# The list scheduler counts with half a microsecond more from the issue of a load to its landing

## The chip, the cores and the metric

The kernel runs on one core of a Trainium2 chip. The metric is the device time of one execution in microseconds (us), lower is better. Each time is that of a whole launch; the profile adds the span from the first to the last instruction of one execution.

## The reference

One inference step of a hybrid encoder layer in float32, for 2,048 prompt tokens and 32 sample tokens (2,080 columns together), width 1,024, feed-forward width 4,096.

```python
sh1, sc1, gt1, sh2, sc2, gt2 = jnp.split((silu(c) @ ada_w[l] + ada_b[l])[:, None, :], 6, axis=-1)
h = rmsnorm(x, norm_mix_g[l]) * (1 + sc1) + sh1
p = h @ w_in                      # u, v | q, k, v | z | a, b
a_out = u * (W_s v + b_s)         # gelu(u), rmsnorm(gelu(v)), chunks of 128 tokens
o, s_new = gated_delta_rule(q, k, vv, beta, g, s0)   # 4 heads, chunked, after a conv of width 4
b_out = rmsnorm(o, dn_norm_g) * silu(z)
x = x + gt1 * (jnp.concatenate([a_out, b_out], axis=-1) @ w_out)
h = rmsnorm(x, norm_ffn_g[l]) * (1 + sc2) + sh2
x = x + gt2 * (jnp.square(jax.nn.relu(h @ w_up[l])) @ w_down[l])
y = rmsnorm(x, final_norm_g)
```

## The kernel before

All large products are made as three matmuls: each float32 operand is split into a rounded high part and the remainder (`split`: ACT rounds, DVE subtracts), and high by high, high by low and low by high are summed in PSUM. A weight block arrives by a transfer into a raw buffer (`raw`, L1420; names `wr`, `s`), ACT writes its high part (`wh`, or `s` for the second feed-forward weight) with an ACTIVATE at L337, and DVE the low part (`wl`) with a TENSOR_TENSOR at L352. In what follows a **conversion** is such an ACT operation on a 128x512 block that a transfer brought, and an **eviction** is an ACT or DVE operation that reads a PSUM result of the feed-forward (names `f`).

The program runs through these stages: a start that makes the modulation from `ada_w` and the first projection (about 0 to 60 us), the mixers in two halves of 1,024 and 1,056 tokens (to about 1,035 us), and the feed-forward in four blocks of 520 tokens (`NB`), the first of which works out sums of weight quadrants (a Strassen scheme with seven products in place of eight) and stores them in DRAM as `su_d` and `sd_d`. Blocks 1 to 3, about 1,400 to 2,400 us, load those sums: 256 KB each, already split for the first weight (so ACT only rounds `wh` and `wl`), and not split for the second. Eight raw buffers of 256 KB serve the loads of blocks 1 to 3; a buffer comes free when ACT and DVE have read it.

No order of instructions is written by hand. Every operation is recorded with an engine, a cost, and what it reads and writes; `Program.schedule` (L237) then plays the program forward in a model of time and gives each engine a fixed order: at each free moment of an engine it takes, among the operations that are ready in the model, the one with the lowest key (priority class, then the earliest GEMM that depends on it). The engines then run these orders as queues: an operation that must wait holds up all that stand behind it on its engine. All transfers, loads and stores, are issued by SP (L390) in the scheduler's DMA order, and an issue whose buffer is not free yet holds up those behind it.

A transfer enters the model through `dma`: it takes the DMA lane for its bytes over 360 (in ns; at least 500), and what depends on it is ready `lat` later. The number that changes stands in `lat`:

```python
x = b / 360
self.p.op(DMA, max(500, x), ..., lat=DMA_LATENCY + min(0, x - 500))
...
s.ready = max(s.ready, end + o.lat + LATENCY.get((o.eng, s.eng), 0.0))
```

So for 256 KB (262,144 bytes) the model counts 728 + 3,000 = 3,728 ns from issue to landing, for 512 KB 4,456 ns, for the 130 KB of a 128x260 tile 3,370 ns. The same `lat` is counted for a store, before its buffer may be written again or its data loaded again.

Of the kernel before, what the change touches and what calls it, by code (L numbers as in the profile page):

```python
# [40 lines left out]
PE, DVE, ACT, POOL, DMA, NONE = range(6)  # L41
TABLES = {AF.Silu: "silu", AF.Gelu_apprx_tanh: "gelu", AF.Exp: "exp", AF.Ln: "ln"}

DMA_LATENCY = 3000


LATENCY = {(PE, DVE): 230, (PE, ACT): 230, (PE, POOL): 230, (DVE, PE): 380, (DVE, DVE): 130, (DVE, ACT): 160,
# [141 lines left out]
def R(x):  # L189
    return x.ap if isinstance(x, View) else x  # L190
# [132 lines left out]
class Kern:  # L323
# [61 lines left out]
    def dma(self, out, in_, n=None):  # L385
# [3 lines left out]
        x = b / 360  # L389
        self.p.op(DMA, max(500, x), lambda: nc.sync.dma_start(out=R(out), in_=R(in_)), [out], [in_], lat=DMA_LATENCY + min(0, x - 500))  # L390

# [1454 lines left out]
```

## Time and profile before

| what | value |
|---|---|
| median of 3 runs | 2415.27 us (2406.06 to 2415.52) |
| the profiled execution's own time | 2432.54 us |
| its span, first to last instruction | 2430.8 us |
| PE busy | 2363.7 us, 97% of the span |
| DVE, ACT, POOL busy | 1728.4, 1551.2, 757.9 us |
| moved by transfers | 570.38 MB, 235 GB/s on the mean |
| granted clock of PE | 0.996 of full |

The profiled execution took 17.27 us longer than the median run. PE is busy nearly throughout, so what another order can change is the 67.1 us of the span in which PE shows no work, and whatever new idle time it makes. Matmuls are pipelined and their ends are modelled, so gaps shorter than a matmul's own length are not seen as idle.

### The profile page before, as it was taken

The numbers are of one execution on the slowest core, as the hardware profiler recorded it, in microseconds if no ns is written. First come the engines' busy times: TensorE is split into PE (matmuls) and PEld (weight loads), VectorE is DVE, ScalarE is ACT, GpSimd is POOL, SyncE is SP. The second block draws the span as 40 slices with busy tenths as digits, with TensorE's granted clock in tenths as the row PEclk, the third lists the DMA queues.
The fourth block names the chain that finished last, engine by engine and source line by source line (L and its number), as shares of the span: only waits on it lengthen the run. The fifth ranks groups of instructions, "written<-read, shape, count | busy, mean of one in ns | idle before, by whom it ended". The sixth has DMA issues, their size and how long they took to land.

```text
span 2430.8 us, 53532 instructions
## 1 busy us (share of the span) xinstructions
PE 2363.7 (97%) x18834; PEld 2209.3 (91%) x18834; DVE 1728.4 (71%) x3993; ACT 1551.2 (64%) x3705; POOL 757.9 (31%) x1055
## 2 busy tenths in 40 slices
PE   7999999999999999999999999999999999999998
PEld 4877778999989878999999999999999999999998
DVE  5556666556664646477777778889788878878796
ACT  4555556465655435365554688777897877877774
POOL 2134523212433223444434353323431212511111
PEclk9999999999999999999999999999999999999999
DMA  8688668455557767888766778786888878876773
GB/s 302 212 280 301 199 192 262 136 180 163 149 167 218 240 189 240 267 266 257 274 217 218 256 245 275 235 292 231 271 284 275 273 237 263 256 251 224 244 232 111
DMA packets 387238, 570.38 MB, mean 235 GB/s; under 512 B 71356, under 2 KB 201296, under 8 KB 386968
## 3 DMA queue, kind: packets, MB, share of 16 engines
q1 hardware_dynamic: 386968, 566.96, 72.5%
q8 instruction: 148, 2.42, 0.4%
q14 instruction: 122, 1.00, 0.1%
HBM read 432.44 MB, written 134.35 MB: 233 GB/s over the span
## 4 chain that ended last, share of the span: by engine, by line
PE 55%; DMA 17%; ACT 9%; DVE 9%; issue 5%; POOL 3%; SPq 1%; DVEq 0%; POOLq 0%; ACTq 0%
PE f L398 25%; PE g L398 22%; DVE s L352 5%; ACT s L337 5%; DMA s<-su_d 4%; PE C L398 3%; POOL s L352 2%; DMA s<-w_u 2%; ACT wh L337 2%; PE B L398 2%; DVE wl L352 1%; DVE s L357 1%; PE L L398 1%; SPq L390 1%; ACT wl L337 1%
## 5 line engine op out<-in xcount | busy, mean ns | idle before, releaser
L337 ACT ACTIVATE s<-s 128x260 fp32r<-128x260 f32 (+9 forms) x1379 | 601.6, 463 | 300.4 <-DVE s L357 82.0
L398 PE MATMUL f<-s,s 128*128 128x260 f32 x4068 | 541.3, 283 | 6.5 <-DVE s L352 4.9
L352 POOL TENSOR_TENSOR s<-s,s 128x260 f32<-128x260 f32 (+3 forms) x354 | 358.5, 1024 | 532.7 <-ACT s L337 400.1
L398 PE MATMUL f<-BH,wh 128*128 128x260 f32 x1796 | 511.1, 285 | 12.7 <-DVE s L352 11.1
L398 PEld LDWEIGHTS f<-s,s 128*128 128x128 f32 x4068 | 508.7, 188 | 11.0 <-DVE s L352 7.2
L398 PE MATMUL f<-BH,wl 128*128 128x260 f32 x1796 | 507.7, 283 | 1.1 <-DVE wl L352 1.1
L398 PE MATMUL f<-BL,wh 128*128 128x260 f32 x1796 | 506.4, 282 | 0.1
L352 DVE TENSOR_TENSOR s<-s,s 128x512 fp32r<-128x512 f32 (+5 forms) x721 | 412.3, 586 | 97.6 <-ACT s L337 63.4
L398 PE MATMUL g<-BH,wh 128*128 128x512 f32 (+2 forms) x1112 | 422.2, 380 | 0.0
L352 DVE TENSOR_TENSOR s<-f,s 128x260 f32<-128x260 f32 x856 | 345.0, 420 | 97.9 <-PE f L398 90.3
L398 PE MATMUL g<-BH,wl 128*128 128x512 f32 (+2 forms) x1112 | 392.9, 353 | 0.0
L398 PE MATMUL g<-BL,wh 128*128 128x512 f32 (+2 forms) x1112 | 391.6, 352 | 0.6 <-DVE BL L352 0.6
L398 PEld LDWEIGHTS f<-BH,wh 128*128 128x128 f32 x1796 | 337.7, 188 | 16.7 <-DVE s L352 8.2
L398 PEld LDWEIGHTS f<-BH,wl 128*128 128x128 f32 x1796 | 338.2, 188 | 1.9 <-DVE wl L352 1.9
L398 PEld LDWEIGHTS f<-BL,wh 128*128 128x128 f32 x1796 | 338.5, 188 | 0.3 <-DVE BL L352 0.3
L352 POOL TENSOR_TENSOR s<-s 128x260 f32<-128x260 f32 (+11 forms) x315 | 155.2, 493 | 475.7 <-DVE s L352 239.5
L337 ACT ACTIVATE wh<-s 128x512 fp32r<-128x512 f32 (+1 forms) x369 | 230.3, 630 | 78.6 <-DMA s<-w_u 28.3
L398 PEld LDWEIGHTS g<-BH,wh 128*128 128x128 f32 x1112 | 211.1, 190 | 26.6 <-issue 9.5
L398 PEld LDWEIGHTS g<-BH,wl 128*128 128x128 f32 x1112 | 210.2, 189 | 19.4
L398 PE MATMUL f<-BH,s 128*128 128x260 f32 x1016 | 225.5, 284 | 0.9 <-DVE s L352 0.8
L398 PEld LDWEIGHTS g<-BL,wh 128*128 128x128 f32 x1112 | 211.1, 190 | 15.0 <-DVE BL L352 1.1
L357 DVE SCALAR_TENSOR_TENSOR s<-s,s,s 128x512 f32<-128x512 f32 (+6 forms) x318 | 164.2, 533 | 76.0 <-ACT s L337 38.4
(119 smaller groups left out, 3537.7 us busy)
## 6 DMA issues: line engine op xcount, KB each, us to landing
s<-su_d SPq DMA_DIRECT2D x288, 256.0 KB, 3.9
s<-w_u SPq DMA_DIRECT2D x171, 256.0 KB, 4.2
s<-w_d SPq DMA_DIRECT2D x151, 256.0 KB, 4.2
s<-sd_d SPq DMA_DIRECT2D x106, 256.0 KB, 4.1
wr<-su_d SPq DMA_DIRECT2D x96, 256.0 KB, 4.4
wr<-w_b SPq DMA_DIRECT2D x42, 512.0 KB, 4.7
wr<-w_d SPq DMA_DIRECT2D x70, 256.0 KB, 4.8
s<-x_d SPq DMA_DIRECT2D x128, 130.0 KB, 3.9
```

The costliest lines, as they stand in the source:

```text
L337: self.p.op(ACT, c, lambda: nc.scalar.activation(out=R(out), in_=R(in_), func=func, **{k: R(v) for k, v in kw.items()}), [out, accum], [in ...
L352: self.p.op(eng, c, lambda: e.tensor_tensor(out=R(out), in0=R(a), in1=R(b), op=op), [out], [a, b])
L357: self.p.op(DVE, c, lambda: nc.vector.scalar_tensor_tensor(out=R(out), in0=R(a), scalar=R(s), in1=R(b), op0=op0, op1=op1), [out], [a, s, b])
L390: self.p.op(DMA, max(500, x), lambda: nc.sync.dma_start(out=R(out), in_=R(in_)), [out], [in_], lat=DMA_LATENCY + min(0, x - 500))
L398: nc.tensor.matmul(R(out), R(l), R(r), **kw)
```

## The change

One constant. It changes the cost of no operation and takes none away; it moves the moment at which the scheduler holds a transfer's data to be there by 500 ns, for every transfer, and with it the order that each engine is given.

```diff
-DMA_LATENCY = 3000
+DMA_LATENCY = 3500
```

The model now counts 4,228 ns for 256 KB, 4,956 ns for 512 KB and 3,870 ns for 130 KB. All five engines' orders change; the instructions are the same ones, except that the change needs 37 loads of ACT's function tables where before has 39. From the first feed-forward eviction on, ACT has 1,011 operations on 128x512 blocks in both programs; the k-th of them stands behind 1.68 more of the other ACT operations in the change than in before, on the mean over all k.

The first place is on ACT, in block 1 of the feed-forward, the stretch that the trace shows from 1552 us on. `wl<-s_405`, `wh<-s_426` and `wl<-s_406` are conversions, `s_427<-s_427` are Relu and Square on a hidden tile, `BH_78<-...` is the split of such a tile, `s_427<-f_18035` is an eviction. Before:

```order
L337 ACTIVATE wl<-wr_96 128x512
L337 ACTIVATE s_411<-s_411,modc,a_90 128x260
L337 ACTIVATE wl<-s_405 128x512
L337 ACTIVATE s_427<-s_427 128x260
L337 ACTIVATE wh<-s_426 128x512
L337 ACTIVATE s_427<-s_427 128x260
L337 ACTIVATE wl<-s_406 128x512
L337 ACTIVATE s_427<-s_427 128x260
L337 ACTIVATE BH_78<-s_427 128x260
L337 ACTIVATE s_427<-s_427 128x260
L337 ACTIVATE BH_78<-s_428 128x260 x2
L337 ACTIVATE s_427<-f_18035 128x260
```

The same place on ACT in the change, where the eviction is called `s_427<-f_18039`:

```order
L337 ACTIVATE wl<-wr_96 128x512
L337 ACTIVATE s_411<-s_411,modc,a_90 128x260
L337 ACTIVATE s_427<-s_427 128x260
L337 ACTIVATE wl<-s_426 128x512
L337 ACTIVATE s_427<-s_427 128x260 x2
L337 ACTIVATE BH_78<-s_427 128x260
L337 ACTIVATE s_427<-s_427 128x260
L337 ACTIVATE s_427<-f_18039 128x260
L337 ACTIVATE BH_78<-s_428 128x260
L337 ACTIVATE s_427<-s_427 128x260
L337 ACTIVATE s_10909<-s_427 128x260
L337 ACTIVATE BH_78<-s_428 128x260
```

Before, three conversions stand between the modulation (`modc`) and the eviction, with ten operations in all between the two; in the change one conversion and six operations stand there, and the other conversions come behind the eviction and the splits.

The second place is on SP, in the start, the stretch that the trace shows from about 25 to 40 us. `ada` are the 512 KB blocks of the modulation weight, `w_b` the first projection's weight, `w_v` the next stage's. Before:

```order
L390 DMA s_408<-ada 128x1024
L390 DMA s_411<-w_b 128x1024
L390 DMA s_405<-ada 128x1024
L390 DMA s_406<-ada 128x1024
L390 DMA s_407<-ada 128x1024
L390 DMA s_408<-ada 128x1024
L390 DMA wr_96<-w_v 128x1040
L390 DMA s_411<-w_v 128x1040
```

The same place on SP in the change:

```order
L390 DMA s_408<-ada 128x1024
L390 DMA wr_96<-w_v 128x1040
L390 DMA s_411<-w_b 128x1024
L390 DMA s_405<-ada 128x1024
L390 DMA s_406<-ada 128x1024
L390 DMA s_407<-ada 128x1024
L390 DMA s_408<-ada 128x1024
L390 DMA s_409<-xT 128x512
L390 DMA s_411<-w_v 128x1040
```

The first block of `w_v` is now issued ahead of the last block of `w_b` that the first projection needs, and ahead of the last four `ada` blocks.

## Rows read from the trace of the kernel before

**Rows 1.** The page's head: span, and PE's line of busy time.

```profile
span 2430.8 us, 53532 instructions
PE 2363.7 (97%) x18834; PEld 2209.3 (91%) x18834; DVE 1728.4 (71%) x3993; ACT 1551.2 (64%) x3705; POOL 757.9 (31%) x1055
```

**Rows 2.** Five stages: length, busy time of each engine, PEclk, DMA share, GB/s.

```profile
0.00:440.00 440.00, 418.19 (x2956) 324.88 (x2959) 266.28 (x679) 246.31 (x604) 139.56 (x242) 1.00 0.76 246
440.00:1000.00 560.00, 551.62 (x4516) 505.95 (x4506) 331.88 (x959) 287.49 (x775) 157.87 (x351) 0.99 0.63 191
1000.00:1140.00 140.00, 131.23 (x980) 128.16 (x979) 101.35 (x174) 81.28 (x188) 66.43 (x54) 0.99 0.85 272
1140.00:1400.00 260.00, 257.75 (x2142) 256.82 (x2141) 192.14 (x365) 142.51 (x323) 101.74 (x82) 1.00 0.72 240
1400.00:2400.00 1000.00, 982.96 (x8086) 972.42 (x8085) 821.70 (x1776) 785.96 (x1800) 281.98 (x312) 1.00 0.78 252
```

**Rows 3.** The chain that ended last, by engine, share of the span.

```profile
PE 55%; DMA 17%; ACT 9%; DVE 9%; issue 5%; POOL 3%; SPq 1%; DVEq 0%; POOLq 0%; ACTq 0%
```

**Rows 4.** Waits of PE from 1400 to 2400 us: total us, times, longest.

```profile
PE f L398 <- DVE s L352: 11.2, 19, 1.6
```

**Rows 5.** DMA issues of the whole span: count, KB each, median us to landing.

```profile
s<-su_d SPq DMA_DIRECT2D x288, 256.0 KB, 3.9
s<-w_u SPq DMA_DIRECT2D x171, 256.0 KB, 4.2
s<-ada SPq DMA_DIRECT2D x16, 512.0 KB, 7.1
```

**Rows 6.** Waits of ACT from 1400 to 2400 us: total us, times, longest.

```profile
ACT s L337 <- PE f L398: 52.0, 65, 2.3
...
ACT wl L337 <- DMA s<-su_d: 27.6, 36, 1.9
ACT wh L337 <- DMA s<-w_u: 22.9, 25, 2.9
ACT wh L337 <- DMA s<-su_d: 15.2, 21, 2.2
```

**Rows 7.** ACT in order of time from 1551 us: start, length, instruction, [idle before].

```profile
1552.55 0.59 ACT L337 ACTIVATE s<-s,modc,a 128x260 f32<-128x260 f32 x1
1553.80 0.63 ACT L337 ACTIVATE wl<-s 128x512 fp32r<-128x512 f32 x1 [0.66 <-DMA s<-su_d]
...
1556.00 0.41 ACT L337 ACTIVATE s<-s 128x260 f32<-128x260 f32 x1
1556.31 0.41 ACT L337 ACTIVATE BH<-s 128x260 fp32r<-128x260 f32 x1
```

**Rows 8.** A piece of the chain that ended last: start, us, what.

```profile
1548.38 5.32 DMA s<-su_d
```

**Rows 9.** Waits of SP's queue from 1400 to 2400 us.

```profile
SPq L390 <- DVE s L352: 278.1, 304, 9.3
```

**Rows 10.** The start in order of time: SP, ACT and PE.

```profile
32.26 0.33 SPq L390 DMA_DIRECT2D s<-w_b  x1
...
37.70 1.06 ACT L337 ACTIVATE wh<-s 128x1024 fp32r<-128x1024 f32 x1 [1.60 <-DMA s<-w_b]
...
76.17 1.03 PE L398 MATMUL B<-s,s 128*2 128x512 f32 x4 [1.64 <-DMA s<-adaw]
```

**Rows 11.** Group of ACT's table loads: busy us, mean ns, idle before.

```profile
L337 ACT ACT_TABLE_LOAD x39 | 50.0, 1283 | 1.4 <-PEq L1839 0.7
```

**Rows 12.** PE after its longest stall past the start, and two windows of 5 us there.

```profile
707.43 0.30 PE L398 MATMUL B<-s,s 32*32 32x16 f32 x5 [3.75 <-issue]
...
705.00:710.00 5.00, 2.57 (x13) 2.35 (x13) 1.49 (x5) 1.78 (x5) 0.00 (x0) 0.57 0.05 12
710.00:715.00 5.00, 5.00 (x46) 4.72 (x46) 2.32 (x6) 3.75 (x10) 0.00 (x0) 0.75 0.38 108
```

## The prediction, before the change was run

> **What bounds the kernel now.** I read the page's head first: PE is busy 2363.7 of 2430.8 us [rows 1]. A new order takes no matmul away, so the most it could give back is the 67.1 us that PE stands idle. The windows by stage say where these lie [rows 2]: 440.00 - 418.19 = 21.8 us up to 440 us, 8.4 us up to 1000, 8.8 us where the feed-forward begins (1000 to 1140), 2.3 us in its block 0, and 1000.00 - 982.96 = 17.0 us in blocks 1 to 3. The remaining 8.8 us are the end of the last block, after its last large product, and hold no weight load.
>
> The chain that ended last goes through transfers for 17% of the span and through PE for 55% only [rows 3]. So although PE is nearly always busy, what it works on has often been released by a load that came just in time. The waits of PE in blocks 1 to 3 name DVE as the releaser, 19 times for 11.2 us [rows 4], 0.6 us each; behind DVE stands ACT, and behind ACT the load: there ACT waits 27.6 + 22.9 + 15.2 = 65.7 us in 36 + 25 + 21 = 82 waits for loads of the first feed-forward weight, 0.80 us each, and 52.0 us in 65 waits for PE's results [rows 6]. These two kinds of wait pull in opposite directions, and the change trades one for the other.
>
> **The change, part by part.**
>
> Is the new number nearer to what happens? The trace has the 256 KB loads land 3.9 to 4.2 us after their issue in the median [rows 5]. The model counted 3.73 us and now counts 4.23. Before, it was short by 0.17 to 0.47 us; now it is right or 0.33 us long. The loads that matter are the late ones: the chain holds one of 5.32 us [rows 8], 1.59 over the old count and 1.09 over the new. The 512 KB loads of the start take 7.1 us in the median [rows 5] against 4.46 and now 4.96, so there both numbers are wrong by over 2 us.
>
> A page of the Trainium skill speaks against the change here. "DMA: Bandwidth & Descriptors", section "Anatomy of one DMA", fits a transfer issued by gpsimd as 2.0 us plus its bytes over 436 GB/s, which as an estimate is 2.6 us for 256 KB. By that the old count was already 1.1 us too long and the change would only delay conversions. These loads are issued by SP, and the trace's 3.9 to 4.2 us [rows 5] disagrees with the figure; the measurement decides.
>
> First term, waits that go away. In the stretch shown, ACT stands 0.66 us at `wl` for a load [rows 7], with Relu, Square, splits and one eviction behind it that need no load. In the change the first Relu stands ahead of that place, two conversions drop behind, and the eviction has six operations ahead of it since the modulation in place of ten. An ACT operation on a 128x260 tile takes 0.31 us from start to start (1556.00 to 1556.31) [rows 7], so the mean displacement of 1.68 operations is 0.52 us, just the number that was added. What of this reaches the end is bounded by PE's idle time in the feed-forward, 8.8 + 2.3 + 17.0 = 28.1 us [rows 2]: the term lies between 0 and -28. Much of it cannot be had by order alone. SP waits 278.1 us in 304 waits for DVE [rows 9], to let go of a buffer or to finish what is to be stored, before it may issue: a load that was issued late lands late whatever ACT does in the meantime. I take a good fifth, **-6 us**, nearer to zero because the 82 waits of ACT cost 65.7 us and PE's named waits only 11.2.
>
> Second term, conversions that come later than they could. ACT's 82 waits are few beside 1,011 such operations in the feed-forward: most loads had landed before their conversion's turn, and there a later place is pure delay, 0.52 us. It costs nothing while the converted block waits for PE, which is the rule, since PE stops so seldom. It costs where PE stops already: if each of the 19 waits on DVE [rows 4] grew by 0.52 us, it would be 9.9 us; if every one of the 65 places where ACT waits for PE [rows 6] became such a stop for 0.52 us, 33.8. Bounds 0 and +34; I take four stops, **+2.1 us**, nearer to zero, since an eviction that moves ahead also gives PE its bank back earlier.
>
> Third term, the start. The last `w_b` block was issued at 32.26 us and ACT waited 1.60 us for it until 37.70 [rows 10]. It now has 520 KB (532,480 bytes) of `w_v` ahead of it; at the stage's 246 GB/s [rows 2] that is 2.2 us. PE has modulation products to fill in, but none of its idle time is spare for the transfers, and later it waits for a load again (1.64 us at 76.17) [rows 10]. Bounds 0 and +2.2, taken at the middle: **+1.1 us**.
>
> Parts priced at nothing. Two table loads of 1.283 us fewer on ACT [rows 11] are 2.6 us of an engine that is busy 246.31 + 287.49 of the first 1000 us [rows 2]; PE covers it (bound -2.6). Stores also count 0.5 us more, so that the model reuses their buffers later; SP's issues then stand later in the order, behind others that are waiting anyway (inside the second term's bounds). The mixers' order changes everywhere, but PE loses only 8.4 us between 440 and 1000.
>
> Sum: -6 + 2.1 + 1.1 = -2.8 us on the profiled execution's 2432.54, that is 2429.7, or a ratio of 0.9988. That execution stands 17.27 us above the median; the ratio on the median of 2415.27 gives **2412 us**.
>
> **The rivals.** A change of 0.5% (12.1 us) is about what a measurement here can tell from none; the three runs of before alone span 9.5 us.
>
> *Faster.* Correcting the count puts evictions and splits ahead of most late loads, and PE's idle time in the feed-forward goes by more than half: -16 us of the 28.1, with the start at +1.1, gives -14.9 us on 2432.54, or 2400 us on the median. For it: the added half microsecond is about what the old count lacked, and ACT's wait of 0.80 us each is of that size. Against: SP's waits [rows 9], and that ACT's waits for PE would have to stay at 52.0 us.
>
> *Slower.* A conversion that ACT could have done on time stands behind an eviction that waits for PE, and PE then stands for the weight block. The place is blocks 1 to 3; the price is 0.52 us per stop. From about 30 stops on it decides: 30 x 0.52 = 15.6 us, with the start +16.7, gives 2449.2 on the profiled execution and **2432 us** on the median. For it: most conversions found their load landed. Against: PE's 17.0 us in 1000 [rows 2] show blocks mostly ready ahead of PE.
>
> *Gaps that cool PE.* At 703.7 us PE stood 3.75 us; in the next two windows its granted clock was 0.57 and 0.75 of full [rows 12], between its two levels of 2.4 and 1.2 GHz. The busy time lost is (1 - 0.57) x 2.57 + (1 - 0.75) x 5.00 = 2.4 us, so such a gap costs 6.2 us in all. Another order can drop one or make one; two more are +12.4 us, with the other terms +9.6, or 2425 us. The Trainium skill, "TensorE: Matmul & The Clock Gate", Part 1, says that an idle array falls to half clock; the trace agrees in these rows.
>
> *The count doesn't matter.* Loads in transfer-bound stretches (512 KB at 7.1 us [rows 5]) come late by more than either count, orders differ but waits do not: 2415 us, inside the forecast's band.
>
> **How the numbers follow.** The forecast with "doesn't matter" holds 0.50, for a time within 0.5% (2403 to 2427). Faster by the first rival 0.27; slower by conversions 0.17; by gaps, two or more of them with some stops, 0.06. Most of the 0.27 lies between 2390 and 2403, since -25.4 us on the profiled execution, most of the 28.1, would be 2390; the slower cases reach 2434. So the range is 2390 to 2434, leaving out about 1 in 10 on either side. Faster 0.27, same 0.50, slower 0.23.
>
> **What would show it.** In blocks 1 to 3 ACT's three waits for loads should fall from 65.7 to about 45 us, its wait for PE's results rise above 52.0, and PE's idle time come to between 10 and 17 us. In the start the `w_v` issue stands before `w_b`'s last, and ACT's wait for that block grows to 3 us or so. If ACT's waits for loads fall but PE's idle time does not, the first term was mis-sized. If PE's idle time in blocks 1 to 3 grows to over 30 us, the second term decides. It is wrong in kind if the time moves in the mixers, where I priced nothing.

## The result, and the profile after

| | before | the change |
|---|---|---|
| median | 2415.27 us (2406.06 to 2416.77, 5 runs) | **2387.63 us** (2384.64 to 2390.38, 5 runs) |
| ratio | 1 | **0.9887**, 95% interval 0.9869 to 0.9906 |
| profiled execution | 2432.54 us, span 2430.8 | 2384.64 us, span 2382.9 |

The change makes the kernel 27.6 us faster, 1.1%. The forecast was 2412 us with "no measurable change" as the likeliest case; the time lies below the range too, by 2.4 us. The two profiled spans differ by more, 47.9 us, because the profiled execution of before took 17.3 us more than its median and that of the change 3.0 us less than its own. So before was profiled once more (c0_before, span 2418.4 us), and below it stands beside [rows 1 to 12] wherever a size matters. Against it the difference is 35.5 us, still 7.9 us more than the medians differ by. The two profiles of before differ by 12.4 us between themselves, so the sizes of stages below, read from single executions, are uncertain by some microseconds.

The page's head of the change: span, busy time of each engine. And its chain that ended last:

```profile
span 2382.9 us, 53525 instructions
...
PE 2342.0 (98%) x18834; PEld 2203.8 (92%) x18834; DVE 1722.2 (72%) x3993; ACT 1543.3 (65%) x3703; POOL 752.3 (32%) x1055
...
PE 79%; DVE 6%; DMA 6%; ACT 4%; issue 3%; POOL 2%; SPq 0%; POOLq 0%; DVEq 0%; ACTq 0%
```

The chain now runs through PE for 79% of the span where it was 55%, and through transfers for 6% where it was 17% [rows 3] (56% and 16% in the second profile of before): what PE works on is released less often by a load that came just in time. Note the busy time of PE. It is 21.7 us less than before [rows 1], although the 18,834 matmuls are the same.

The windows by stage in the change (length, then busy us and count of PE, PEld, DVE, ACT and POOL, granted clock, DMA share, GB/s):

```profile
0.00:440.00 440.00, 420.71 (x2920) 332.38 (x2923) 267.35 (x683) 244.72 (x604) 136.25 (x243) 1.00 0.76 247
440.00:1000.00 560.00, 554.25 (x4647) 511.56 (x4635) 334.05 (x967) 292.53 (x783) 165.46 (x359) 1.00 0.64 200
1000.00:1140.00 140.00, 135.74 (x1064) 133.25 (x1063) 111.21 (x192) 87.36 (x203) 71.54 (x56) 1.00 0.83 271
1140.00:1400.00 260.00, 260.00 (x2168) 259.42 (x2167) 189.09 (x365) 149.28 (x342) 105.45 (x94) 1.00 0.72 240
```

Windows of fixed times show little here: PE's idle time fell by 2.5, 2.6, 4.5 and 2.3 us against [rows 2], but the stages themselves have moved. What tells more is where each stage ends. I mark the end of the mixers by the start of the last matmul of the projections (tile `g`) and the ends of the feed-forward's blocks by the start of the last row of small matmuls against a column of ones (`M<-ones`) of each:

| stage | before, first profile | before, second profile | the change |
|---|---|---|---|
| start and mixers, to | 1046.1 us | 1043.2 | 1027.3 |
| block 0 | 368.9 | 363.4 | 362.3 |
| blocks 1 to 3 | 1005.0 | 1001.0 | 983.7 |
| the rest | 10.8 | 10.8 | 9.6 |

Against the second profile the 35.5 us are 15.9 + 1.1 + 17.3 + 1.2: nearly half lies in the mixers, where the forecast had priced nothing. Blocks 1 to 3 in windows of their own, cut at whole microseconds, first in the change, then in before, then in the second profile of before:

```profile
1390.00:2373.00 983.00, 979.18 (x8128) 975.45 (x8128) 826.20 (x1794) 778.52 (x1797) 279.39 (x310) 1.00 0.78 256
```

```profile
1415.00:2420.00 1005.00, 987.38 (x8122) 976.79 (x8120) 826.39 (x1794) 783.07 (x1796) 280.49 (x311) 1.00 0.77 250
```

```profile
1407.00:2408.00 1001.00, 987.68 (x8120) 976.94 (x8119) 823.04 (x1793) 784.15 (x1795) 281.07 (x311) 1.00 0.77 251
```

The idle time that PE shows is 17.6 us and 13.3 us before, 3.8 us after, so it fell by 13.8 or 9.5 us. But the stage became 22 or 18 us shorter. The rest is in PE's *busy* time, 987.4 and 987.7 before, 979.2 after, for the same matmuls. How can that be? It isn't the clock, which is granted at 1.00 of full in all three lines. The groups of the largest kind of matmul there (busy us, mean ns of one), before, then the change:

```profile
L398 PE MATMUL f<-s,s 128*128 128x260 f32 x2916 | 390.4, 283 | 4.2 <-DVE s L352 4.2
```

```profile
L398 PE MATMUL f<-s,s 128*128 128x260 f32 x2916 | 385.9, 283 | 0.4 <-DVE s L352 0.4
```

Each matmul is shown 283 ns long, but they overlap, and 390.4 us over 2,916 of them is 134 ns each. So one that starts some 0.15 us late leaves no gap in the profile, and a longer delay leaves a gap that is about 0.15 us too small. Here such delays hide 4.5 us in one group, beside the 3.8 us that show.

The waits of ACT in the change from 1400 to 2400 us (total us, times, longest), then those of PE and of SP's queue:

```profile
ACT s L337 <- PE f L398: 59.4, 74, 2.3
...
ACT wh L337 <- DMA s<-su_d: 11.2, 18, 1.4
...
ACT wl L337 <- DMA s<-su_d: 10.3, 15, 1.7
...
ACT wh L337 <- DMA s<-w_u: 9.1, 12, 2.2
...
PE f L398 <- DVE s L352: 2.7, 5, 0.9
...
SPq L390 <- DVE s L352: 266.4, 299, 4.7
```

ACT's three waits for loads fell from 65.7 us to 10.3 + 11.2 + 9.1 = 30.6 us, its wait for PE's results rose from 52.0 to 59.4 us [rows 6], and PE's waits on DVE fell from 11.2 to 2.7 us [rows 4]. SP still waits 266.4 us for DVE, against 278.1 [rows 9].

At the first place shown under the change, ACT in order of time (start, length, instruction, [idle before]):

```profile
1521.94 0.63 ACT L337 ACTIVATE wl<-wr 128x512 fp32r<-128x512 f32 x1 [0.90 <-DMA wr<-su_d]
1522.74 0.61 ACT L337 ACTIVATE s<-s,modc,a 128x260 f32<-128x260 f32 x1 [0.16 <-DVE s L352]
1523.25 0.41 ACT L337 ACTIVATE s<-s 128x260 f32<-128x260 f32 x1
1523.56 0.62 ACT L337 ACTIVATE wl<-s 128x512 fp32r<-128x512 f32 x1
...
1525.32 0.36 ACT L337 ACTIVATE s<-f 128x260 f32<-128x260 f32 x1
```

The wait of 0.66 us behind the modulation [rows 7] is gone, the one conversion left there finds its block landed, and the eviction starts 2.58 us after the modulation. A wait of 0.90 us for another load stands ahead of the place: single waits remain, their number went down.

The start, SP, ACT and PE in order of time in the change:

```profile
30.53 0.42 SPq L390 DMA_DIRECT2D wr<-w_v  x1
...
32.95 0.33 SPq L390 DMA_DIRECT2D s<-w_b  x1
...
38.70 1.04 ACT L337 ACTIVATE wh<-s 128x1024 fp32r<-128x1024 f32 x1
...
72.21 1.03 PE L398 MATMUL B<-s,s 128*2 128x512 f32 x4 [0.34 <-DMA s<-adaw]
```

`w_v` is issued ahead of `w_b`'s last block, as the order said. ACT converts that block 1.00 us later than before [rows 10] with no wait shown, and PE's later stop in the modulation is 0.34 us where it was 1.64. Neither size belongs to the order alone: in the second profile of before ACT waits 3.79 us for that block and converts it at 38.24 us, and PE's two last stops there are 0.65 and 0.27 us.

### The profile page after: what moved, and what is told of

Same layout as the page of the kernel before. It is cut to its first block, busy times and chain, and to the rows that moved or that the text cites. A ratio compares the mean times of both kernels' runs of the same rounds, so it can differ in the third digit from the quotient of the medians.

```text
span 2382.9 us, 53525 instructions
## 1 busy us (share of the span) xinstructions
PE 2342.0 (98%) x18834; PEld 2203.8 (92%) x18834; DVE 1722.2 (72%) x3993; ACT 1543.3 (65%) x3703; POOL 752.3 (32%) x1055
## 4 chain that ended last, share of the span: by engine, by line
PE 79%; DVE 6%; DMA 6%; ACT 4%; issue 3%; POOL 2%; SPq 0%; POOLq 0%; DVEq 0%; ACTq 0%
PE f L398 43%; PE g L398 27%; PE C L398 3%; DVE s L352 3%; ACT s L337 2%; PE B L398 2%; POOL s L352 2%; PE L L398 1%; PE M L398 1%; DVE wl L352 1%; DVE s L357 1%; PE L L409 1%; ACT wh L337 1%; DMA s<-su_d 1%; DVE BL L352 1%
## 5 line engine op out<-in xcount | busy, mean ns | idle before, releaser
L337 ACT ACTIVATE s<-s 128x260 f32<-128x260 f32 (+8 forms) x1379 | 601.5, 463 | 327.9 <-DVE s L357 90.7
L398 PE MATMUL f<-s,s 128*128 128x260 f32 x4068 | 535.5, 283 | 0.4 <-DVE s L352 0.4
L352 DVE TENSOR_TENSOR s<-s,s 128x512 fp32r<-128x512 f32 (+5 forms) x721 | 402.6, 572 | 64.6 <-ACT s L337 42.1
L357 DVE SCALAR_TENSOR_TENSOR s<-s,s,s 128x400 f32<-128x400 f32 (+6 forms) x318 | 164.2, 532 | 57.2 <-ACT s L337 36.4
```

Of the source, the lines that this page charges most:

```text
L337: self.p.op(ACT, c, lambda: nc.scalar.activation(out=R(out), in_=R(in_), func=func, **{k: R(v) for k, v in kw.items()}), [out, accum], [in ...
L352: self.p.op(eng, c, lambda: e.tensor_tensor(out=R(out), in0=R(a), in1=R(b), op=op), [out], [a, b])
L357: self.p.op(DVE, c, lambda: nc.vector.scalar_tensor_tensor(out=R(out), in0=R(a), scalar=R(s), in1=R(b), op0=op0, op1=op1), [out], [a, s, b])
L398: nc.tensor.matmul(R(out), R(l), R(r), **kw)
```

## The experiments

Two theories. **Count**: the number itself matters. With the longer landing the model stops putting conversions ahead of loads that haven't come, and ACT, DVE and PE stop less; the time must then vary smoothly with the number, and through the loads. **Shuffle**: any change of the number makes another order among thousands of near ties, and this one happened to be good; then ten nanoseconds would move the time as much as five hundred. All ratios are to before on the same chip, with 95% intervals.

### Where it comes from: feed-forward or mixers

`e1_ffn` counts 3,500 only for what the feed-forward records; `e2_mix` has the two numbers the other way round.

```diff
+        self.lat = 3000
...
-        ..., lat=DMA_LATENCY + min(0, x - 500))
+        ..., lat=self.lat + min(0, x - 500))
...
+            self.lat = 3500
             self.feed_forward()
```

> The 500 ns more are counted only for transfers recorded in the feed-forward; the start and the mixers keep 3,000. Count theory (the number gains because conversions no longer stand ahead of their loads): the feed-forward's part of the gain comes back, ratio 0.990 to 0.994, and PE's idle time in blocks 1 to 3 falls from 17 us to under 8. Shuffle theory (another order is only another draw): a ratio anywhere from 0.985 to 1.01, without a tie between PE's idle time and ACT's waits for loads.

> The 500 ns more are counted only for the start and the mixers; the feed-forward keeps 3,000. Count theory: the remaining part of the gain, ratio 0.994 to 0.998, the feed-forward's idle time as before; this run and the one of the feed-forward alone add up to the change's -1.1%. Shuffle theory: no such sum.

Measured: e1_ffn 0.9921 (0.9891 to 0.9950), 2405.80 us; e2_mix 0.9943 (0.9923 to 0.9964), 2410.23 us. Each stage gains by itself, 0.8% and 0.6%, and neither gain is given back in the other stage. Their sum, 1.4%, is more than the change's 1.1%, by no more than the intervals allow. Blocks 1 to 3 in e1_ffn, then in e2_mix:

```profile
1409.00:2395.00 986.00, 980.02 (x8130) 975.79 (x8130) 825.97 (x1795) 779.66 (x1798) 281.25 (x310) 1.00 0.79 255
```

```profile
1396.00:2400.00 1004.00, 989.82 (x8140) 979.83 (x8139) 825.29 (x1794) 782.08 (x1797) 281.59 (x311) 1.00 0.77 250
```

They are short where the feed-forward counts 3,500, and as long as in before where it doesn't; the mixers end at 1047.3 us in e1_ffn and at 1029.1 in e2_mix.

### Loads or stores

`e3_loads` counts 3,500 for transfers into SBUF and 3,000 for stores, `e4_stores` the reverse.

```diff
+        load = isinstance(out, View) and not out.mem.dram
-        ..., lat=DMA_LATENCY + min(0, x - 500))
+        ..., lat=(3500 if load else 3000) + min(0, x - 500))
```

> 3,500 for transfers into SBUF, 3,000 for stores to DRAM. Count theory: nearly the whole gain, ratio 0.987 to 0.992, since the waits that went were for loads. If the stores' count carries the gain (buffers and stored sums that are held back longer), 0.997 to 1.003.

> 3,000 for loads, 3,500 for stores to DRAM. Count theory for loads: no change, 0.997 to 1.003. If the stores carry the gain: 0.987 to 0.993. Shuffle theory: both this and the loads alone somewhere between 0.985 and 1.01.

Measured: e3_loads 0.9871 (0.9839 to 0.9903), 2393.58 us; e4_stores 0.9978 (0.9959 to 0.9996), 2416.82 us. The loads' count carries the gain; the stores' count is worth 0.2%, hardly more than its interval.

### The number itself

```diff
-DMA_LATENCY = 3000
+DMA_LATENCY = 2500     (s1_2500; 3250, 4000 and 4500 in s2, s3 and s4)
```

> The count the other way: 2,500 in place of 3,000 (256 KB: 3.23 us, 0.7 to 1.0 us short of the median landing). Count theory: slower than before by 0.5 to 1.5%, and ACT's waits for loads in blocks 1 to 3 grow past 99 us, to 130 or more. Shuffle theory: as likely faster as slower, within 1%.

> Half the step. Count theory: about half the gain, ratio 0.991 to 0.997, ACT's waits for loads between 52 and 99 us. Shuffle theory: no order between this and the neighbours.

> Twice the step (256 KB: 4.73 us, above the median landing of 3.9 to 4.2, below the late ones of 5 to 6). Count theory: at least the change's gain, 0.982 to 0.990 against before, since late loads are still uncovered; ACT's waits for loads under 52 us. My second term (conversions later than they could be) says the gain turns here: 0.990 to 0.997, with ACT's waits for PE above 64 us and PE idle more.

> Three times the step (256 KB: 5.23 us, about the late loads). Count theory: between 0.982 and 0.992; from here on the count is longer than nearly all landings, so no more is won. Second term: slower than the change by 0.5% or more, since each conversion stands a microsecond behind its load.

| count, ns | ratio, 95% interval | mixers end, us | blocks 1 to 3, us | PE idle there | ACT's waits there for any load (times) |
|---|---|---|---|---|---|
| 2,500 | 1.0176 (1.0139 to 1.0213) | 1061.8 | 1027.6 | 28.9 | 138.4 (161) |
| 3,000 (two profiles) | 1 | 1046.1, 1043.2 | 1005.0, 1001.0 | 17.6, 13.3 | 99.0 (128), 100.5 (138) |
| 3,250 | 0.9895 (0.9877 to 0.9913) | 1027.5 | 993.7 | 9.0 | 76.8 (104) |
| 3,500, the change | 0.9887 (0.9869 to 0.9906) | 1027.3 | 983.7 | 3.8 | 52.3 (91) |
| 4,000 | 0.9901 (0.9883 to 0.9919) | 1042.8 | 981.7 | 2.0 | 37.0 (59) |
| 4,500 | 0.9942 (0.9924 to 0.9960) | 1052.7 | 980.3 | 2.2 | 23.6 (39) |

The curve has a flat bottom from 3,250 to 4,000, and nearly the whole gain comes with the first 250 ns. Not all of this was expected. At 2,500 the loss is larger than the 1.5% that the count theory allowed, and 3,250 was to bring half of the gain. At 4,000 and 4,500 the ratios lie just outside the count theory's bands and inside those of the second term, but the second term's signs are missing: over blocks 1 to 3 ACT waits 47.9 us and 59.6 us for PE's results (`s` from `f`), not above 64, and PE is idle less.

The two ends of the curve have different causes. At 2,500 blocks 1 to 3 are long, and ACT waits for loads (the waits of ACT there: total us, times, longest):

```profile
ACT wh L337 <- DMA s<-su_d: 33.1, 38, 2.8
...
ACT wh L337 <- DMA s<-w_u: 24.6, 25, 2.9
...
ACT wl L337 <- DMA s<-su_d: 21.3, 28, 2.1
```

At 4,500 those blocks have reached their floor of some 980 us: the window holds 978.78 us of PE's work.

```profile
1414.00:2395.00 981.00, 978.78 (x8142) 976.32 (x8140) 831.18 (x1796) 774.40 (x1799) 282.31 (x311) 1.00 0.79 256
```

What is lost there is lost in the mixers, near the end of the second half. PE in order of time in s4_4500:

```profile
937.71 0.69 PE L409 MATMUL C<-ident,s 128*128 128x128 f32 x2 [1.48 <-DVE s L366]
...
950.18 0.69 PE L409 MATMUL C<-ident,s 128*128 128x128 f32 x2 [1.89 <-DVE s L366]
...
969.96 0.31 PE L409 MATMUL C<-ident,s 32*128 32x32 f32 x1 [1.30 <-DVE s L366]
973.73 0.70 PE L398 MATMUL g<-BH,wh 128*128 128x400 f32 x1 [3.46 <-ACT BH L337]
```

Small steps of the delta rule lie bare here: a small matmul waits for DVE, and the next large product for ACT, with nothing in PE's queue ahead of them to fill the time. These four stops are 8.13 us; the mixers end 25.4 us later than in the change.

Much of the rest is PE's clock. Behind two shorter stops (0.46 us ahead of 934.17 and 0.64 ahead of 935.52) it falls to the lower of its two levels (1.2 of 2.4 GHz), and it falls again among the later ones. Two windows of s4_4500, then the only such stretch that the change has before the end of its mixers (length, busy us and count of PE, PEld, DVE, ACT and POOL, granted clock, DMA share, GB/s):

```profile
936.00:958.00 22.00, 14.18 (x51) 11.25 (x50) 10.04 (x32) 6.60 (x20) 4.25 (x6) 0.53 0.50 161
967.00:978.00 11.00, 6.00 (x22) 4.89 (x23) 6.68 (x17) 4.98 (x11) 5.06 (x6) 0.53 0.88 267
```

```profile
949.00:954.00 5.00, 4.81 (x24) 4.49 (x23) 2.96 (x7) 3.54 (x7) 2.44 (x3) 0.66 0.80 255
```

Counted as the prediction counts it, the busy time lost is (1 - 0.53) x (14.18 + 6.00) = 9.5 us against (1 - 0.66) x 4.81 = 1.6 us in the change; two shorter stretches, at 25 and 718 us, add some 4.5 us to the 9.5. So some 12 us of the 25.4 are the clock, as an estimate, and PE's visible idle time up to the mixers' end is 15.2 us longer, 40.2 where the change has 25.0. Together that is about the loss, even a little more. All four executions of s4_4500 show a lower mean clock, 0.990 to 0.992 of full, than those of the change, 0.995 to 0.998.

### Ten nanoseconds

```diff
-DMA_LATENCY = 3000
+DMA_LATENCY = 2990     (c1_2990; 3510 in c2_3510)
```

> Only 10 ns less than before: the count is the same for any purpose, but PE's order alone differs in 20,683 lines. Count theory: 0.996 to 1.006 against before, ACT's waits for loads in blocks 1 to 3 between 85 and 115 us. Shuffle theory: 0.985 to 0.995, as easily as the change got it, by another draw.

> 10 ns more than the change, another order in 23,116 lines on PE. Count theory: 0.985 to 0.993 against before, ACT's waits for loads between 40 and 65 us, blocks 1 to 3 within 981 to 988 us. Shuffle theory: back to 0.995 to 1.005.

Measured: c1_2990 1.0001 (0.9987 to 1.0014), 2422.66 us beside 2423.58; c2_3510 0.9886 (0.9870 to 0.9903), 2396.06 us. Both times are those of their neighbours. How much of the order did 10 ns move? How the two expectations counted their lines isn't recorded. By tile names without buffer numbers and by shapes, in the order of the traces, PE has another matmul at 2,738 of its 18,834 places in c1_2990 than in before, and at 3,266 in c2_3510 than in the change; between before and the change it is 5,793. So by this count 10 ns move about half as much as 500 ns do, and none of the time. e4_stores says it more strongly: it differs from before at 4,804 places, nearly as much as the change, and is 0.2% faster.

The mixers' ends say the same. The six profiles in which the mixers' loads count 3,000 or 2,990 end them at 1040.9 to 1047.5 us, with four clearly different orders on PE among them; the six with 3,500 or 3,510 end them at 1026.9 to 1032.2, with three. **Shuffle** falls: the order is another one and the time is the same, as long as the count is about the same.

> The kernel before once more, for a second trace of the same order. If the stages' lengths belong to the order: mixers 1044 to 1049 us, blocks 1 to 3 between 990 and 1008, PE's stall of about 4 us at 705 us again. If the first profiled execution was a slow draw: blocks 1 to 3 some 10 us shorter than 1005.

This is the second profile of before that is used throughout: one run of 2420.15 us, span 2418.4. Blocks 1 to 3 (1001.0 us) came as expected, and the stop at 705 us came again, with 2.68 us; the mixers ended at 1043.2 us, just below the band.

### The mixers' share

`g1_start` counts 3,500 in the start only, `g2_mixonly` in the mixers only.

```diff
+        self.lat = 3500          (g2_mixonly: 3000)
...
         self.startup()
+        self.lat = 3000          (g2_mixonly: 3500, and 3000 again ahead of feed_forward)
```

> 3,500 counted only for the transfers recorded in the start (modulation weight, first projection, constants), 3,000 for the mixers and the feed-forward. If the start carries the mixers' gain: ratio 0.993 to 0.997, the mixers end at 1027 to 1033 us. If the third term was right (w_v ahead of w_b costs): 1.000 to 1.002, the mixers end at 1044 to 1049.

> 3,500 counted only for the transfers recorded in the mixers, 3,000 for the start and the feed-forward. If the mixers proper carry the gain: ratio 0.992 to 0.997, the mixers end at 1027 to 1034 us. If the start carries it: 0.998 to 1.002.

Measured: g1_start 0.9985 (0.9971 to 0.9999), 2418.09 us; g2_mixonly 0.9958 (0.9938 to 0.9978), 2409.73 us. Together they are e2_mix's 0.6%. The mixers' own transfers carry most of it: they end at 1030.7 us in g2_mixonly, as expected, and at 1040.9 in g1_start, which fits neither of the two cases expected for it.

### A number for each stage

The curve suggests 3,500 for start and mixers, where 4,000 already costs, and 4,500 for the feed-forward, which is at its floor there.

```diff
+        self.lat = 3500
...
+            self.lat = 4500
             self.feed_forward()
```

> 3,500 in the start and the mixers, 4,500 in the feed-forward: each stage with the number at which it was shortest. Count theory: blocks 1 to 3 in 980 to 984 us, the mixers as in the change, ratio 0.984 to 0.990; no clear gain over the change, since PE has only a few us of idle time left in the feed-forward. Shuffle theory: no better than 0.990 to 1.0.

Measured: **0.9840** (0.9823 to 0.9857), 2386.44 us; on the same chip c2_3510, in effect the change, took 2396.06 us. So this version beats both kernels, the change by some 0.4% (2386.44 over 2396.06 is 0.996; c2_3510's runs span 2392.50 to 2399.38, this one's 2380.96 to 2389.99), where I had expected no clear gain over the change. Blocks 1 to 3, and ACT's waits in them:

```profile
1395.00:2376.00 981.00, 978.53 (x8137) 975.90 (x8136) 832.99 (x1796) 774.90 (x1799) 280.75 (x311) 1.00 0.80 256
```

```profile
ACT wh L338 <- DMA s<-su_d: 6.6, 8, 1.7
...
ACT wh L338 <- DMA s<-w_u: 6.1, 6, 2.0
...
ACT wl L338 <- DMA s<-su_d: 3.0, 5, 0.9
```

The three waits are down to 15.7 us in 19 times, PE's idle time to 2.5 us, and the mixers end at 1030.9 us.

## Why the prediction was wrong

**In the feed-forward the bottleneck and the mechanism were right.** Late loads hold ACT, behind it DVE and then PE; the longer count moves evictions and splits ahead of them, and the waits go. ACT's waits for loads and the length of blocks 1 to 3 fall together through all the counts in the table, from 138.4 us and 1027.6 us to 23.6 us and 980.3. That the loads themselves came sooner is not the reason: c2_3510 has the change's gain with the landing times of before (last section).

**Two steps failed: the size of the first term, and the mixers at nothing.** The first term was put at -6 us; measured are -21.3 us against the profile that the sum was made on, and -17.3 us against the second one, in blocks 1 to 3 alone. Three things were wrong in it.

- *How far the waits fall.* I forecast the three waits of ACT to go from 65.7 to about 45 us; they went to 30.6. And I had left out the rest: over blocks 1 to 3, with the loads of the second weight, ACT waits for loads 99.0 and 100.5 us before and 52.3 after, 47 or 48 us less where I counted on 21. The price was too low as well. I had implied 6 us for 20.7, or 0.29 us of the end for each microsecond of the three waits. They fell by 35.1 us against the first profile and by 31.0 against the second (24.1 + 21.4 + 16.1 = 61.6 us there), so the price was 21.3 / 35.1 = 0.61 or 17.3 / 31.0 = 0.56.
- *The argument from SP.* I held that a load issued late lands late whatever the order, because SP waits 278.1 us for DVE [rows 9]. SP's wait hardly fell (266.4 us), and yet the stops went. What mattered, as I read it, was whether ACT stood in front of a block that hadn't come, or did something else until it had.
- *The bound.* I took the idle time that PE shows, 17.0 us in 1,000 [rows 2], as the most that blocks 1 to 3 could give. They gave 21.3 us while only 13.8 us of visible idle time went; in the second profile, which shows 13.3 us, they gave 17.3. Delays below some 0.15 us are busy time in the profile. For the whole feed-forward I had put the bound at 28.1 us; against the first profile it gave 21.3 + 6.6 + 1.2 = 29.1, against the second 17.3 + 1.1 + 1.2 = 19.6.

**"Priced at nothing: the mixers' order" was wrong.** They ended 15.9 to 18.8 us earlier, and e2_mix and g2_mixonly show that it is mostly the count for their own transfers that does it. The prediction had called itself wrong in kind if the time moved there, and nearly half of the gain did. I had looked at PE's visible 8.4 us between 440 and 1000 us and stopped there. What I can place: PE's visible idle time up to the mixers' end fell from 32.8 and 32.3 us to 25.0. Measured from start to start of PE's matmuls, against the median distance of the same pair of shapes, the excess of all distances that are over 0.25 us too long sums to 38.6 and 34.4 us before and 23.3 after, so 11 to 15 of the 16 to 19 us are gaps. Some 3 to 4 us more are the clock. Before, it stood at its lower level in three stretches ahead of the mixers' end, by the windows around them:

```profile
705.00:713.00 8.00, 5.57 (x25) 5.33 (x25) 2.70 (x10) 3.65 (x9) 0.00 (x0) 0.57 0.15 43
842.00:846.00 4.00, 4.00 (x15) 3.35 (x15) 0.42 (x2) 0.37 (x1) 0.00 (x0) 0.57 0.95 259
1033.00:1037.00 4.00, 4.00 (x16) 3.50 (x15) 1.85 (x3) 1.77 (x4) 1.69 (x3) 0.57 0.54 168
```

The busy time lost is (1 - 0.57) x (5.57 + 4.00 + 4.00) = 5.8 us, as an estimate; in the second profile two stretches make 4.9, in the change the one shown above 1.6. ACT's waits for loads up to the mixers' end fell from 60.2 and 65.0 to 49.0 us, DVE's from 35.7 and 36.2 to 14.8. Which of these waits sets the mixers' end was not taken apart, and stays open.

**The second term** (conversions later than they could be, +2.1 us): no run shows a cost in the feed-forward. Even with 1.5 us more in the count, blocks 1 to 3 are at their shortest. The mixers do lose from 4,000 on, but the stops shown there wait for DVE's small steps and ACT's split, not for a converted weight block, so that loss isn't shown to be this one.

**The third term** (the start, +1.1 us): the order of issues came as forecast, the price didn't. ACT's wait for `w_b`'s last block, forecast at 3 us or so, is not there at all, though ACT converts the block 1.00 us later than in the first profile and 0.46 later than in the second. g1_start is 0.15% faster, at the edge of what its interval can tell.

**The rivals.** *Faster* was the right one, though ACT's wait for PE, which it wanted to stay at 52.0 us, rose to 59.4. Its time, 2400 us, was too long for the same reasons, and it too held nothing of the mixers. *Slower* is refuted by the result, and by all counts from 3,250 to 4,500. *Gaps that cool PE* named something real that worked the other way here: the change has less time at the lower clock than before, which is worth the 3 to 4 us above, and at 4,500 the clock costs some 12. The stop that it started from doesn't decide the time. It shows again in the second profile of before and in e1_ffn, as PE's rows show (c0_before, then e1_ffn):

```profile
705.03 0.24 PE L398 MATMUL B<-s,s 32*32 32x16 f32 x5 [2.68 <-issue]
```

```profile
709.27 0.29 PE L399 MATMUL B<-s,s 32*32 32x16 f32 x5 [4.60 <-issue]
```

The change has no such stop, but neither has c1_2990, whose mixers end at 1047.5 us all the same. *The count doesn't matter* falls with the scan.

**The page that spoke against the change.** The fit in "DMA: Bandwidth & Descriptors" of the Trainium skill, "Anatomy of one DMA", is for transfers that gpsimd issues; as an estimate it gives 2.6 us for 256 KB, and by it even the count of 2,500 would have been long enough. The runs here disagree: s1_2500, with 3.23 us for 256 KB, is 1.8% slower than before, and for these loads, issued by SP, the traces' own landing times were the better guide.

## What to carry to other kernels

In a kernel whose order a planner fixes, don't count a load as landing sooner than the median one does; somewhat later costs little. Here 256 KB landed in 3.9 to 4.2 us in the median; counts of 4.0 to 4.7 us for it (3,250 to 4,000 in the number) were worth 1% against 3.7, and of the numbers tried 1 us less than the change's cost 2.9% where 1 us more cost 0.6%. Scan the number, and scan it apart for each stage: here the feed-forward did best with the longest that was tried, 4,500 ns, and the mixers with their bare chain of small steps lost from 4,000 on. And don't take an engine's visible idle time as the most that a better order can give: measure how far apart its instructions start, or the length of the whole stage, and look at the waits of the engines behind it, also where it seems never to stop. And read the granted clock of each stage beside its stops: where stops crowd, part of the price is the clock behind them.

## What the runs showed beyond that

Did the loads land sooner in the change, so that fewer waits need no other reason? The DMA issues of the change (count, KB each, median us to landing), then two of c2_3510, which is as fast:

```profile
s<-su_d SPq DMA_DIRECT2D x288, 256.0 KB, 3.7
s<-w_u SPq DMA_DIRECT2D x171, 256.0 KB, 3.8
...
s<-ada SPq DMA_DIRECT2D x16, 512.0 KB, 5.2
```

```profile
s<-su_d SPq DMA_DIRECT2D x288, 256.0 KB, 4.0
s<-w_u SPq DMA_DIRECT2D x171, 256.0 KB, 4.1
```

The 256 KB loads of the change are 0.2 and 0.4 us shorter than in [rows 5], those of c2_3510 are not. Over all sixteen profiles the medians of these two kinds lie between 3.7 and 4.4 us and show no trend with the count, so the gain doesn't come from sooner landings. The 512 KB loads of the start do differ between orders, 4.3 us in s4_4500 to 7.8 in the second profile of before (7.1 in the first): their landing time read from one order is not a constant to be put into the planner that made it. Why they differ was not tested.

PE's stop of 2.7 to 4.6 us at about 705 us, within a run of matmuls of 32x16, is put down to "issue": by the profile it waits for nothing. It shows in the three profiles that have the same order of matmuls on PE up to the end of the mixers (before, its second profile and e1_ffn). s4_4500 has one of 1.88 us at 718 us, the other twelve have none, so it goes with the order. Its cause isn't shown.
